# Two-layer hybrid trunk: four normalised half tiles and the first attention's queries and keys transposed by transfers, the end of attention reordered, half of one scaling moved to ScalarE

## The chip, the cores and the metric

The kernel runs on one core of a Trainium2 chip. The metric is device time in microseconds (us) of one execution. The kernel before has a median of 1316.64 us over three runs (1316.31 to 1316.8). The execution that the profiler recorded took 1317.49 us; the span from its first to its last instruction is 1315.7 us.

Five engines appear: PE (TensorE, matrix products and transposes), DVE (VectorE), ACT (ScalarE), POOL (GpSimd) and SP (SyncE), whose queue issues nearly all transfers. Each engine executes its own instructions in their program order, and waits at an instruction until what that instruction needs is there.

## The reference

Two layers over 256 tokens of width 1024 in float32. Each layer is a half-weighted SwiGLU block, an attention block with three branches, a second SwiGLU block and a gated embedding. Cut to what matters here:

```python
for i in range(DEPTH):                                    # DEPTH = 2
    h = h + 0.5 * swiglu(rms_norm(h, norm_g[i, 0]), ffn1_wi[i], ffn1_wo[i])
    z = split_cols(rms_norm(h, norm_g[i, 1]) @ w_in[i], IN_SPLITS)
    # z: aq, ak, av | bq, six key/value sets, gates | cq, ck, cv | ga, gb, gc
    ya = diff_attention(aq, ak, av, ...)                  # 4 heads, two maps each
    yb = nsa_attention(bq, ..., sigmoid(bgate), ...)      # compressed + selected + window
    yc = swa_sink_attention(cq, ck, cv, ...)              # window of 128 with sinks
    merged = (sigmoid(ga) * (ya @ w_branch[i, 0]) + sigmoid(gb) * (yb @ w_branch[i, 1])
              + sigmoid(gc) * (yc @ w_branch[i, 2]))
    h = h + merged @ w_out[i]
    h = h + 0.5 * swiglu(rms_norm(h, norm_g[i, 2]), ffn2_wi[i], ffn2_wo[i])
    h = h + sigmoid(rms_norm(h, norm_g[i, 3]) @ w_ple_gate[i]) * (p[i] @ w_ple[i])
return rms_norm(h, final_norm)
```

## The kernel before

The 256 tokens are two row tiles, t = 0 and 1, of 128 tokens. A float32 product is made of three products of shorter operands: each operand is split into a high part and a remainder (`split`, ACT writes the high part at L249, DVE the remainder at L244), and `mul3` (L256 to L258) multiplies high by high, high by remainder and remainder by high. So every pair of a 128-deep block of the left side and 512 columns of weights costs PE three instructions.

**Weights** are streamed in pieces of 128 x 1024 (`load`, L355). One piece is a transfer into one of four `raw` buffers (SP, L361), ACT's `wh` and DVE's `wl`, in six buffers each. All pieces of the program stand in one queue in the order of their use, and a product that reaches a piece has the next two fetched too. `product` (L388) takes tile 0 through its blocks and tile 1 eight blocks behind it; a 1024-deep product of 512 columns has eight blocks, so there tile 0 is done before tile 1 begins. When a tile's sum is complete, `done` is traced at raised priority.

**The order of the instructions** comes from a planner: the program is traced in order, and the planner then simulates the engines and issues, for each engine, what is ready first by its own estimates, with the trace order (moved forward for what is traced at raised priority) as the preference. Buffers of a tag are handed out as they come free. `keep_in_program_order` pins an instruction behind what has been traced before it on its engine. Slow side work (the attention branches) is written as generators in `Flow`: `flow.tick()`, once for every block of a product, lets each lane advance by its pace, and `flow.join` runs a side to its end.

**Transposes.** What is to be the left side of a product must be transposed. In most places PE does it: `transposes` (L264) turns 128 x 128 blocks into a PSUM bank of the tag `tp` (three banks), and ACT and DVE split the result from there. `Norm.turn` does so for half a row tile (four blocks) of `h` after each half of a residual, multiplying by the norm's weight on the way (L429, L430). `toT` (L876) does it for queries and keys: in `done_a` (L941) for the first attention, four blocks for each of two products `A0`, `A1` and each row tile. The SwiGLU blocks use `turn_by_dma` (L529) for their inner activations: ACT copies the float32 tile into two planes of 16-bit halves (`cut`, L535), SP issues a transposing transfer into `flip` (L536), and `collect` puts the halves together again (L541) on ACT or DVE, five steps of the block's line of products later.

**The output products of a SwiGLU block** (`fo`, `run` in `outer`, L810) are made in two halves of 512 columns, c = 0 and 1; behind each half and row tile `residual` (L465) adds to `h`, turns the half tile for the next norm and adds up its squares.

**Attention's end**, in the generators of `attention` and `branch`: for the last branch (b) the gate products of both halves are made, the branch's side is joined for tile 0, `tile(0)` makes the two products with `yB[0]` and mixes them into `merged`, turns them (`mt`, L1333) and splits them into `mT[0]`; then the side is joined to its end and `tile(1)` does the same for tile 1. Then come the output products `wo`, half 0 for both tiles, half 1 for both tiles. Product banks are two of the tag `mm` and two of the tag `s`.

**Scaling in branch b**: after the softmax, `first` in `attend_b` multiplies each head's probabilities by a number per row on DVE (L1228).

Of the kernel before, what the change touches and what calls it, by code (L numbers as in the profile page):

```python
# [11 lines left out]
F32R = mybir.dt.float32r  # L12
# [9 lines left out]
NT = SEQ // 128  # L22
# [11 lines left out]
FIRST, LAST = 7, 3  # L34
SPLIT = 16
POINTS = (5, 8, 11, 14, 18, 21)
PACE_A, PACE_B, PACE_C = 0.75, 0.72, 0.6
# [170 lines left out]
def trunk(ctx: ExitStack, tc: tile.TileContext, a: dict, out: bass.AP, index: list):  # L208
# [60 lines left out]
    class Weights:  # L269


        def __init__(self, width, pieces, per, push=True):
            self.width, self.per, self.pieces = width, per, pieces
            self.tiles, self.at = [None] * len(pieces), [None] * len(pieces)
            if push:
                for j in range(len(pieces)):
                    self.push(j)

        def push(self, j):
            self.at[j] = len(queue)  # L280
            queue.append(lambda: self.tiles.__setitem__(j, load(*self.pieces[j], 2 if self.at[j] < 2 else 1)))

# [88 lines left out]

    def streamed(i, name, width, push=True):
        p, c = where[i, name]
        return Weights(width, [(a["wst"][p + j], SUB) for j in range(c)], SUB // width, push)

# [31 lines left out]
    class Norm:  # L407
# [9 lines left out]
        def turned(self, t, k, src, pin=False):  # L417
# [47 lines left out]
    def residual(norm, c, scale, final=False):  # L465

        s = slice(512 * c, 512 * c + 512)

        def done(t, ps):
            nc.vector.scalar_tensor_tensor(h[:, t, s], ps, scale(t), h[:, t, s], op0=ALU.mult, op1=ALU.add)  # L470
# [58 lines left out]
    def turn_by_dma(pool, src, m):  # L529


        cut = stage("cut").bitcast(U16)[:, :256 * m]
        flip = pool.tile([128, 2, 4, 128], U16, tag="flip", bufs=4, name="flip")
        flip = flip.rearrange("p w a b -> p (w a) b")[:, :2 * m]
# [10 lines left out]
    def ffn(i, n, norm, after, aside=None):  # L545
# [4 lines left out]
        def begin():  # L550
            nonlocal pool
            pool = phase("ffn")
            for t in range(NT):
                gT[t] = pool.tile([128, 2, NF, 128], F32R, name=f"gT{t}")
# [307 lines left out]
    def attention(i, norm, after):  # L862
# [3 lines left out]
        def begin():  # L866
            nonlocal pool
            pool = phase("attn")
            wide[0] = False
            for t in range(NT):  # L870
                merged[t] = pool.tile([128, D], F32, name=f"merged{t}")
# [4 lines left out]
        def toT(dst, t, blocks, srcs):  # L876

            ps = tp_bank("qt")
            transposes(ps, srcs)
            v = ps[:, :len(srcs) * 128].rearrange("p (k q) -> p k q", q=128)  # L880
            ts = slice(t * 128, (t + 1) * 128)
            split(dst[:, 0, blocks, ts], dst[:, 1, blocks, ts], v)

        def scores(name, q, qb, t, key):
# [56 lines left out]
        def done_a(m):  # L941
            def done(t, ps):
# [4 lines left out]
                nc.vector.tensor_scalar(sb[:, 256:], ps[:, 256:], norm.r(t), None, op0=ALU.mult)  # L947
                toT(qk[m], t, slice(0, 4), [sb[:, 128 * k:128 * k + 128] for k in range(4)])
            return done
# [61 lines left out]
        def done_bk(t, ps):  # L1011
# [3 lines left out]
            for c in range(2):  # L1015
# [3 lines left out]
                nc.scalar.activation(dst[:, :, 0, :], src, AF.Copy, scale=norm.r(t))  # L1019
                nc.vector.tensor_scalar(dst[:, :, 1, :], src, norm.r(t), None, op0=ALU.mult)  # L1020
                srcs = [sb[:, k * 128:(k + 1) * 128] for k in range(4)]
# [7 lines left out]
                else:  # L1029
                    toT(kB[0], t, slice(0, 4), srcs)  # L1030

# [14 lines left out]
        def done_q(dst, name):  # L1046
            def done(t, ps):
# [3 lines left out]
                nc.scalar.activation(sb, ps, AF.Copy, scale=norm.eighth(t))  # L1051
                toT(dst[0], t, slice(0, 4), [sb[:, 128 * k:128 * k + 128] for k in range(4)])
            return done
# [144 lines left out]
        def attend_b():  # L1198
            bnd, y_ps = {}, {}

            def first(u):
# [25 lines left out]
                for j in range(n):  # L1227
                    nc.vector.tensor_scalar(pr[j], pr[j], st[:, 2 * n + j:2 * n + j + 1], None, op0=ALU.mult)  # L1228
                yield
                return p  # L1230

            def second(u, p):
# [12 lines left out]
                if ss[-1] == 1:  # L1245
# [4 lines left out]
                    weighted(y_ps[g, t], vc[0][:, 0], T.rearrange("p x j q -> p x (j q)"), False, True)  # L1250
                    gather(yB[t], y_ps[g, t], g)
                    readyB[t] += 1
# [7 lines left out]
        def done_ck(t, ps):  # L1260
# [6 lines left out]
            nc.scalar.activation(dst[:, :, 0, :], src, AF.Copy, scale=norm.r(t))  # L1267
            nc.vector.tensor_scalar(dst[:, :, 1, :], src, norm.r(t), None, op0=ALU.mult)
            toT(kC[0], t, slice(0, 2), [sb[:, 0:128], sb[:, 128:256]])
            values(vC[0][:, t], ps[:, 128:256], norm.r(t))  # L1270
# [43 lines left out]
        def branch(b, yT, side, last=False):  # L1314
# [69 lines left out]
        def start(name, side, pace, lane=0):  # L1384
            sides[name] = flow.start(side, pace, lane)

        yield lambda: start("a", attend_a(), PACE_A)
        yield project("Ck", done_ck, 256)
        yield project("Cq", done_q(qC, "qC"))
        yield project("Bk", done_bk)  # L1390
        yield lambda: start("c", attend_c(), PACE_C)
        wbv = a["wbv"][i]
# [3 lines left out]
        yield from branch(0, yA, "a")  # L1396
        yield second_weights
        yield lambda: start("b", attend_b(), PACE_B)
        w1 = streamed(i, "w1", 256)
# [120 lines left out]

    opened = []

    def phase(name):
# [3 lines left out]
        opened.append(stack)  # L1527
        return stack.enter_context(tc.tile_pool(name=name, bufs=1, reuse_waits="tile"))

# [73 lines left out]
```

## Time and profile before

| | |
|---|---|
| median of three runs | 1316.64 us (1316.31 to 1316.8) |
| profiled execution | 1317.49 us, span 1315.7 us |
| PE busy | 1300.9 us, 99% of the span, 6306 instructions |
| PE's weight loads | 1072.7 us, 82% |
| DVE busy | 1098.3 us, 83%, 1778 instructions |
| ACT busy | 890.6 us, 68%, 1412 instructions |
| POOL busy | 29.1 us, 2% |
| chain that ended last | PE 95%, DVE 2%, issue 1%, ACT 1% |
| DMA | 259.55 MB, mean 197 GB/s |

A row of the groups view names the line, the engine and the operation, then what is written and read (`out<-in`), the shape and the number of instructions; behind the bar stand the busy time, the mean time of one and the time that the engine sat idle before them, with what ended it. The busy time of PE counts overlapping instructions once. A matmul of 512 columns shows 0.39 us from its start to its modelled end, but the next one starts 0.23 us after it, so what an instruction costs PE is read from the starts of its neighbours in the timeline.

### The profile page before, as it was taken

The numbers are of one execution on the slowest core, as the hardware profiler recorded it, in microseconds if no ns is written. First come the engines' busy times: TensorE is split into PE (matmuls) and PEld (weight loads), VectorE is DVE, ScalarE is ACT, GpSimd is POOL, SyncE is SP. The second block draws the span as 40 slices with busy tenths as digits, with TensorE's granted clock in tenths as the row PEclk, the third lists the DMA queues.
The fourth block names the chain that finished last, engine by engine and source line by source line (L and its number), as shares of the span: only waits on it lengthen the run. The fifth ranks groups of instructions, "written<-read, shape, count | busy, mean of one in ns | idle before, by whom it ended". The sixth has DMA issues, their size and how long they took to land.

```text
span 1315.7 us, 18006 instructions
## 1 busy us (share of the span) xinstructions
PE 1300.9 (99%) x6306; PEld 1072.7 (82%) x6306; DVE 1098.3 (83%) x1778; ACT 890.6 (68%) x1412; POOL 29.1 (2%) x46
## 2 busy tenths in 40 slices
PE   9999999999999999999999999999999999999997
PEld 7888888887887788888888888888888878888886
DVE  7878976768979799997799999677688888999975
ACT  6777555658857577874667875566695656877654
POOL 0000000000000000000000000000000000000000
PEclk9999999999999999999999999999999999999999
DMA  8778775346653567786666796744556436677762
GB/s 309 231 227 267 206 223 203 116 161 188 217 165 109 169 184 241 220 224 214 205 193 228 203 248 206 243 154 153 176 159 218 158 96 210 202 212 232 216 223 81
DMA packets 120283, 259.55 MB, mean 197 GB/s; under 512 B 54774, under 2 KB 60278, under 8 KB 120192
## 3 DMA queue, kind: packets, MB, share of 16 engines
q1 hardware_dynamic: 117232, 248.38, 60.7%
q0 software_dynamic: 2528, 9.47, 2.1%
q8 instruction: 49, 0.80, 0.3%
q10 hardware_dynamic: 432, 0.56, 0.1%
q14 instruction: 42, 0.34, 0.1%
HBM read 245.75 MB, written 1.08 MB: 188 GB/s over the span
## 4 chain that ended last, share of the span: by engine, by line
PE 95%; DVE 2%; issue 1%; ACT 1%; DMA 0%; SPq 0%; POOLq 0%; POOL 0%; DVEq 0%; ACTq 0%
PE ff L258 8%; PE ff L257 8%; PE ff L256 8%; PE fo L257 5%; PE fo L258 5%; PE fo L256 5%; PE p L256 4%; PE p L257 4%; PE p L258 4%; PE gate L258 3%; PE gate L256 3%; PE gate L257 3%; PE s L895 2%; PE A L258 2%; PE A L256 2%; PE A L257 2%
## 5 line engine op out<-in xcount | busy, mean ns | idle before, releaser
L249 ACT ACTIVATE wh<-raw 128x1024 fp32r<-128x1024 f32 (+2 forms) x430 | 446.8, 1049 | 208.2 <-DMA raw<-in_wst 63.9
L244 DVE TENSOR_TENSOR wl<-raw,wh 128x1024 fp32r<-128x1024 f32 (+2 forms) x430 | 514.4, 1211 | 85.4 <-ACT wh L249 82.0
L257 PE MATMUL ff<-wl,nT 128*128 128x512 f32 x480 | 187.8, 393 | 0.0
L258 PE MATMUL ff<-wh,nT 128*128 128x512 f32 x480 | 187.4, 392 | 0.2 <-DVE nT L244 0.2
L256 PE MATMUL ff<-wh,nT 128*128 128x512 f32 x480 | 179.8, 394 | 0.6 <-ACT nT L430 0.6
L257 PE MATMUL fo<-wl,gT 128*128 128x512 f32 x304 | 117.7, 390 | 0.0
L258 PE MATMUL fo<-wh,gT 128*128 128x512 f32 x304 | 117.6, 391 | 0.0
L256 PE MATMUL fo<-wh,gT 128*128 128x512 f32 x304 | 114.9, 390 | 0.0
L256 PEld LDWEIGHTS ff<-wh,nT 128*128 128x128 f32 x480 | 90.9, 189 | 20.7 <-ACT nT L430 1.6
L258 PEld LDWEIGHTS ff<-wh,nT 128*128 128x128 f32 x480 | 90.9, 189 | 19.6 <-DVE nT L244 0.8
L257 PEld LDWEIGHTS ff<-wl,nT 128*128 128x128 f32 x480 | 90.9, 189 | 19.5 <-DVE wl L244 0.8
L256 PE MATMUL gate<-wh,nT 128*128 128x512 f32 x192 | 76.8, 400 | 0.0
L257 PE MATMUL gate<-wl,nT 128*128 128x512 f32 x192 | 76.2, 397 | 0.0
L258 PE MATMUL gate<-wh,nT 128*128 128x512 f32 x192 | 76.0, 396 | 0.0
L257 PEld LDWEIGHTS fo<-wl,gT 128*128 128x128 f32 x304 | 57.1, 188 | 12.3 <-DVE wl L244 0.5
L256 PEld LDWEIGHTS fo<-wh,gT 128*128 128x128 f32 x304 | 57.1, 188 | 11.8
L258 PEld LDWEIGHTS fo<-wh,gT 128*128 128x128 f32 x304 | 57.1, 188 | 11.7
L906 ACT ACTIVATE p<-p,st 128x128 f32<-128x128 f32 (+1 forms) x128 | 56.7, 446 | 6.3 <-DVE st L904 6.1
L535 ACT ACTIVATE cut<-gated 128x1024 uint16<-128x1024 uint16 (+1 forms) x48 | 46.1, 975 | 10.0 <-DVE gated L574 8.8
L244 DVE TENSOR_TENSOR wl<-x,wh 128x1024 fp32r<-128x1024 f32 x42 | 50.6, 1221 | 2.3 <-ACT wh L249 2.0
L249 ACT ACTIVATE wh<-x 128x1024 fp32r<-128x1024 f32 x42 | 43.7, 1049 | 6.3 <-DVE x L244 4.6
L257 PE MATMUL p<-wl,xs 128*128 128x512 f32 x112 | 43.6, 389 | 0.0
(377 smaller groups left out, 2719.6 us busy)
## 6 DMA issues: line engine op xcount, KB each, us to landing
raw<-in_wst SPq DMA_DIRECT2D x424, 512.0 KB, 4.4
y<-in_wst POOLq DMA_DIRECT2D x6, 1024.0 KB, 5.8
band<-table SPq DMA_DIRECT2D x10, 512.0 KB, 5.1
xy<-in_wst POOLq DMA_DIRECT2D x4, 512.0 KB, 4.0
raw<-in_wbv SPq DMA_DIRECT2D x4, 420.0 KB, 3.2
xt<-in_xt SPq DMA_DIRECT2D x4, 256.0 KB, 5.5
raw<-in_wst SPq DMA_DIRECT2D x4, 256.0 KB, 5.1
h<-in_x SPq DMA_DIRECT2D x2, 512.0 KB, 7.8
```

What stands on the lines that cost most here:

```text
L244: nc.vector.tensor_tensor(o, x, y, op=ALU.subtract)
L249: nc.scalar.activation(hi, src, AF.Copy)
L256: nc.tensor.matmul(ps, xh, wh, start=start, stop=False, **kw)
L257: nc.tensor.matmul(ps, xh, wl, start=False, stop=False, **kw)
L258: nc.tensor.matmul(ps, xl, wh, start=False, stop=stop, **kw)
L535: nc.scalar.activation(cut.rearrange("p (w n) -> p w n", w=2), halves(src)[:, :128 * m].rearrange("p n w -> p w n"), AF.Copy)
L895: nc.tensor.matmul(o, q[r, x, qb[m], t * 128:(t + 1) * 128], kk, start=x + y == 0, stop=x == 1)
L906: nc.scalar.activation(p[j], p[j], AF.Exp, bias=st[:, j:j + 1], scale=-1.0, accum_out=st[:, n + j:n + j + 1])
```

## The change

The diff has five parts. **(1)** `residual` calls the new `turn_late` for half 0 behind `fo` (norms with odd row numbers: two per layer, two row tiles each): `turn_by_dma` in place of PE's four transposes, and after eight ticks `collect` on ACT and the rest of the norm as before, from SBUF. **(2)** `done_a` calls the new `late_T`, which for `A0` and `A1` does the same with `collect` on DVE; all other callers get `toT` as before. `turned_all` joins these sides ahead of the branches. **(3)** In the last branch the gate of half 1 is made up to all but its last two blocks for tile 1; these two blocks follow the join for tile 1. The output products are traced in a new order, with two blocks of half 1 for tile 0 between the tiles of half 0, and the first two weight pieces of `wo` half 0 lie in buffers of the tag `blk` in place of `wh` and `wl`. `gather` of the last unit of branch b is traced at raised priority. **(4)** Every second scaling of L1228 runs on ACT. **(5)** In `done_bk` and `done_ck` the second copy of the keys is copied from the first one in place of being scaled from PSUM again. The flips of attention use buffers of the tag `th`.

```diff
+TURNS = ('A0','A1')
+ON_DVE = TURNS
+QWAIT = 8
+SHARE = 2
+LEFT = 2
+APART = ((0, 1), ())
+WAIT = 8
+LATE_ON = False
...
-    def load(src, n, parts=1):
+    def load(src, n, parts=1, apart=False):
         raw = base.tile([128, SUB], F32, tag="raw", bufs=RAWS, name="raw")
-        hi = base.tile([128, SUB], F32R, tag="wh", bufs=WBUFS, name="wh")
-        lo = base.tile([128, SUB], F32R, tag="wl", bufs=WBUFS, name="wl")
+        if apart:
+            both = base.tile([128, 2, SUB], F32R, tag="blk", bufs=6, name="wb")
+            hi, lo = both[:, 0], both[:, 1]
+        else:
+            hi = base.tile([128, SUB], F32R, tag="wh", bufs=WBUFS, name="wh")
+            lo = base.tile([128, SUB], F32R, tag="wl", bufs=WBUFS, name="wl")
...
+        def turn_late(self, t):
+            collect = turn_by_dma(current[0], h[:, t, :512], 4)
+            def side():
+                for _ in range(WAIT):
+                    yield
+                with tc.high_priority(offset=150):
+                    self.turned(t, 0, collect(LATE_ON).rearrange("p k q -> p (k q)"))
+                yield
+            flow.start(side(), 1.0, ("nt", t))
...
             if final:
                 finish(t, 0, 512)
+            elif c == 0 and norm.row % 2:
+                norm.turn_late(t)
             else:
                 norm.turn(t, c)
...
+        def late_T(name, dst, t, n, sb):
+            if name not in TURNS:
+                return toT(dst, t, slice(0, n), [sb[:, 128 * k:128 * k + 128] for k in range(n)])
+            collect = turn_by_dma(pool, sb, n)
+            def side():
+                for _ in range(QWAIT):
+                    yield
+                ts = slice(t * 128, (t + 1) * 128)
+                split(dst[:, 0, :n, ts], dst[:, 1, :n, ts], collect(name in ON_DVE))
+                yield
+            turning.append(flow.start(side(), 1.0, ("qt", name, t)))
...
-                toT(qk[m], t, slice(0, 4), [sb[:, 128 * k:128 * k + 128] for k in range(4)])
+                late_T(f"A{m}", qk[m], t, 4, sb)
...
-                nc.vector.tensor_scalar(dst[:, :, 1, :], src, norm.r(t), None, op0=ALU.mult)
+                nc.vector.tensor_copy(dst[:, :, 1, :], dst[:, :, 0, :])
...
                 for j in range(n):
-                    nc.vector.tensor_scalar(pr[j], pr[j], st[:, 2 * n + j:2 * n + j + 1], None, op0=ALU.mult)
+                    of = st[:, 2 * n + j:2 * n + j + 1]
+                    if j % SHARE:
+                        nc.scalar.activation(pr[j], pr[j], AF.Copy, scale=of)
+                    else:
+                        nc.vector.tensor_scalar(pr[j], pr[j], of, None, op0=ALU.mult)
...
             if last:
-                for c in range(2):
-                    yield gated(c, both[c][0])
+                yield gated(0, both[0][0])
+                wg = streamed(i, f"g{'abc'[b]}1", 512)
+                gate_ps = [None] * NT
+                def gates(t, ks):
+                    for k in ks:
+                        if k == 0:
+                            gate_ps[t] = product_bank(f"gate{t}")
+                        mul3(gate_ps[t], *norm.lhs(t, k), *wg(k), k == 0, k == NK - 1)
+                        flow.tick()
+                    if ks[-1] == NK - 1:
+                        with tc.high_priority(offset=150):
+                            both[1][0](t, gate_ps[t])
+                yield lambda: gates(0, range(NK))
+                yield lambda: gates(1, range(NK - LEFT))
                 ws = [streamed(i, f"br{b}{c}", 512) for c in range(2)]
...
                 yield lambda: tile(0)
                 yield lambda: flow.join(sides[side])
+                yield lambda: gates(1, range(NK - LEFT, NK))
                 yield lambda: tile(1)
...
-        for c in range(2):
-            yield product(lambda t, k: (mT[t][:, 0, k, :], mT[t][:, 1, k, :]), NK, after(c), "wo", streamed(i, f"wo{c}", 512))
+        done = [after(c) for c in range(2)]
+        ws = [streamed(i, f"wo{c}", 512, apart=APART[c]) for c in range(2)]
+        def out():
+            ps = {}
+            for c, t, ks in ((0, 0, range(NK)), (1, 0, range(2)), (0, 1, range(NK)), (1, 0, range(2, NK)), (1, 1, range(NK))):
+                for k in ks:
+                    if k == 0:
+                        ps[c, t] = product_bank(f"wo{t}")
+                    mul3(ps[c, t], mT[t][:, 0, k, :], mT[t][:, 1, k, :], *ws[c](k), k == 0, k == NK - 1)
+                    flow.tick()
+                if ks[-1] == NK - 1:
+                    with tc.high_priority(offset=150):
+                        done[c](t, ps[c, t])
+        yield out
```

More of the change, by code (lines that the diff above doesn't have):

```diff
@@ L35 @@
 SPLIT = 16
+TURNS = ('A0','A1')
[6 more added lines that the diff above has]
+LATE_ON = False
+FLIPS = ["flip"]
 POINTS = (5, 8, 11, 14, 18, 21)
@@ L269, in trunk, with __init__ @@
     class Weights:
-        def __init__(self, width, pieces, per, push=True):
-            self.width, self.per, self.pieces = width, per, pieces
+        def __init__(self, width, pieces, per, push=True, apart=()):
+            self.width, self.per, self.pieces, self.apart = width, per, pieces, apart
             self.tiles, self.at = [None] * len(pieces), [None] * len(pieces)
@@ L280, in push @@
             self.at[j] = len(queue)
-            queue.append(lambda: self.tiles.__setitem__(j, load(*self.pieces[j], 2 if self.at[j] < 2 else 1)))
+            queue.append(lambda: self.tiles.__setitem__(j, load(*self.pieces[j], 2 if self.at[j] < 2 else 1, j in self.apart)))
         def __call__(self, k):
@@ L370, in trunk, with streamed @@
         pos += c
-    def streamed(i, name, width, push=True):
+    def streamed(i, name, width, push=True, apart=()):
         p, c = where[i, name]
-        return Weights(width, [(a["wst"][p + j], SUB) for j in range(c)], SUB // width, push)
+        return Weights(width, [(a["wst"][p + j], SUB) for j in range(c)], SUB // width, push, apart)
     def last_product(lhs, nk, done, name, w):
@@ L532, in turn_by_dma @@
         cut = stage("cut").bitcast(U16)[:, :256 * m]
-        flip = pool.tile([128, 2, 4, 128], U16, tag="flip", bufs=4, name="flip")
+        flip = pool.tile([128, 2, 4, 128], U16, tag=FLIPS[0], bufs=4, name="flip")
         flip = flip.rearrange("p w a b -> p (w a) b")[:, :2 * m]
@@ L552, in begin @@
             pool = phase("ffn")
+            FLIPS[0] = "flip"
             for t in range(NT):
@@ L868, in begin @@
             pool = phase("attn")
+            FLIPS[0] = "th"
             wide[0] = False
@@ L882, in toT, with turned_all @@
             split(dst[:, 0, blocks, ts], dst[:, 1, blocks, ts], v)
+        turning = []
+        def late_T(name, dst, t, n, sb):
[9 more added lines that the diff above has]
+            turning.append(flow.start(side(), 1.0, ("qt", name, t)))
+        def turned_all():
+            while turning:
+                flow.join(turning.pop(0))
         def scores(name, q, qb, t, key):
@@ L1029, in done_bk @@
                 else:
-                    toT(kB[0], t, slice(0, 4), srcs)
+                    late_T("Bk", kB[0], t, 4, sb)
         def values(v, ps, scale):
@@ L1051, in done @@
                 nc.scalar.activation(sb, ps, AF.Copy, scale=norm.eighth(t))
-                toT(dst[0], t, slice(0, 4), [sb[:, 128 * k:128 * k + 128] for k in range(4)])
+                late_T(name, dst[0], t, 4, sb)
             return done
@@ L1250, in second @@
                     weighted(y_ps[g, t], vc[0][:, 0], T.rearrange("p x j q -> p x (j q)"), False, True)
-                    gather(yB[t], y_ps[g, t], g)
+                    with tc.high_priority(offset=150 if g == t == 1 else 0):
+                        gather(yB[t], y_ps[g, t], g)
                     readyB[t] += 1
@@ L1267, in done_ck @@
             nc.scalar.activation(dst[:, :, 0, :], src, AF.Copy, scale=norm.r(t))
-            nc.vector.tensor_scalar(dst[:, :, 1, :], src, norm.r(t), None, op0=ALU.mult)
-            toT(kC[0], t, slice(0, 2), [sb[:, 0:128], sb[:, 128:256]])
+            nc.vector.tensor_copy(dst[:, :, 1, :], dst[:, :, 0, :])
+            late_T("Ck", kC[0], t, 2, sb)
             values(vC[0][:, t], ps[:, 128:256], norm.r(t))
@@ L1385, in start @@
             sides[name] = flow.start(side, pace, lane)
+        yield turned_all
         yield lambda: start("a", attend_a(), PACE_A)
@@ L1390, in attention @@
         yield project("Bk", done_bk)
+        yield turned_all
         yield lambda: start("c", attend_c(), PACE_C)
@@ L1397, in attention @@
         yield second_weights
+        yield turned_all
         yield lambda: start("b", attend_b(), PACE_B)
@@ L1519, in setup @@
         yield
-    opened = []
+    opened, current = [], []
     def phase(name):
@@ L1527, in phase @@
         opened.append(stack)
-        return stack.enter_context(tc.tile_pool(name=name, bufs=1, reuse_waits="tile"))
+        current[:] = [stack.enter_context(tc.tile_pool(name=name, bufs=1, reuse_waits="tile"))]
+        return current[0]
     norms = [Norm(n) for n in range(4 * DEPTH + 1)]
```

## The prediction

> **What bounds the kernel now.** I read the page first (engines, groups), then who waited for whom on PE, then PE's timeline at the places that the change touches.
>
> ```profile
> PE 1300.9 (99%) x6306; PEld 1072.7 (82%) x6306; DVE 1098.3 (83%) x1778; ACT 890.6 (68%) x1412; POOL 29.1 (2%) x46
> ```
>
> PE's own waits (time in all, times, longest):
>
> ```profile
> PE wo L256 <- ACT mT L252: 1.4, 2, 0.7
> PE mt L264 <- DVE pT L244: 1.2, 2, 0.6
> ...
> PE gl L1097 <- DVE c_sb L1090: 0.5, 2, 0.3
> ...
> PE wo L256 <- ACT wh L249: 0.5, 2, 0.2
> ```
>
> PE is busy for 1300.9 of 1315.7 us, and nearly all of the remaining 14.8 us lie before the first product and behind the last. The waits inside the program are small; the three around `wo` and `mt` lie at attention's end and are 3.1 us over both layers. So the time is the number of PE instructions times their spacing, and an edit helps only if it takes instructions or waits off PE.
>
> The spacing is read from starts, and so is what a group of four transposes costs:
>
> ```profile
> 179.65 0.62 PE L258 MATMUL fo<-wh,gT 128*128 128x512 f32 x2
> 180.10 0.39 PE L256 MATMUL fo<-wh,gT 128*128 128x512 f32 x1
> 180.34 0.60 PE L264 MATMUL nt<-ident,h 128*128 128x128 f32 x4
> 180.69 0.48 PE L256 MATMUL fo<-wh,gT 128*128 128x512 f32 x1
> ...
> 199.88 0.40 PE L258 MATMUL A<-wh,nT 128*128 128x512 f32 x1
> 200.12 0.60 PE L264 MATMUL qt<-ident,stage 128*128 128x128 f32 x4
> 200.47 0.48 PE L256 MATMUL A<-wh,nT 128*128 128x512 f32 x1
> ...
> 204.91 0.39 PE L257 MATMUL A<-wl,nT 128*128 128x512 f32 x1
> 205.14 0.38 PE L264 MATMUL qt<-ident,stage 128*128 128x128 f32 x2
> 205.28 0.48 PE L258 MATMUL A<-wh,nT 128*128 128x512 f32 x1
> 205.60 0.39 PE L256 MATMUL A<-wh,nT 128*128 128x512 f32 x1
> 205.83 0.38 PE L264 MATMUL qt<-ident,stage 128*128 128x128 f32 x2
> 205.96 0.48 PE L257 MATMUL A<-wl,nT 128*128 128x512 f32 x1
> ```
>
> Two products start 0.45 us before the next, so one takes 0.23. With four transposes between, the next product starts 0.59 us after the last one (180.10 to 180.69, 199.88 to 200.47): the group costs 0.36 us. Split into pairs it costs 0.14 (204.91 to 205.28, less 0.23) and 0.13 (205.60 to 205.96), 0.27 together.
>
> **The change part by part.** Durations are from the profiled execution (1317.49 us, span 1315.7), 0.85 us above the median of the runs; the sum of differences is taken off the median.
>
> *Norm halves.* Two layers, two SwiGLU blocks, two row tiles: 8 groups leave PE, 8 x 0.36 = **-2.9 us**.
>
> *Queries and keys of the first attention.* 2 products x 2 row tiles x 2 layers: 8 groups. In the first layer one is whole and three are in pairs; taking the second layer alike, 2 x (0.36 + 3 x 0.27) = **-2.3 us**. The bounds are all split (-2.2) and all whole (-2.9).
>
> What takes their place runs on ACT, SP and DVE (the view of one tile: shortest, median and longest in ns; the groups; two stretches of the first layer):
>
> ```profile
> L535 ACT ACTIVATE cut<-gated x48: 614/1042/1061, 33.7 to 1222.9; 128x1024 uint16<-128x1024 uint16 x40, 128x512 uint16<-128x512 uint16 x8
> L536 SPq DMA_TRANSPOSE flip<-cut x48: 1189/1239/4823, 34.8 to 1224.3; - x48
> DMA to landing us min/median/max: 3.0/4.2/8.1
> ```
>
> ```profile
> L541 ACT ACTIVATE whole<-flip 128x1024 uint16<-128x1024 uint16 x24 | 32.0, 1364 | 2.9 <-DMA flip<-cut 2.7
> ```
>
> ```profile
> L541 DVE COPY gw<-flip x8: 741/752/756, 125.1 to 1215.7; 128x1024 uint16<-128x1024 uint16 x8
> ```
>
> ```profile
> 157.00:188.00 31.00, 31.00 (x143) 25.60 (x142) 24.04 (x37) 16.24 (x21) 0.15 (x1) 1.00 0.66 204
> 188.00:224.00 36.00, 36.00 (x172) 29.17 (x169) 23.45 (x34) 19.57 (x28) 3.02 (x2) 1.00 0.63 209
> ```
>
> Each late norm half adds 1.04 us of `cut` and 1.36 of `collect` on ACT; each late query tile 1.04 on ACT and 0.75 on DVE. The two stretches (columns: PE, PEld, DVE, ACT, POOL, clock, DMA share, GB/s) hold two of the former and four of the latter: ACT goes to 16.2 + 4.8 = 21.0 of 31 and 19.6 + 4.2 = 23.8 of 36 us, DVE in the second to 23.5 + 3.0 = 26.5 of 36. So idle time of ACT and DVE covers them. SP issues 16 more transfers of 1.24 us, in order with the weights; the same transfers, 48 of them, already stand in that queue. DMA is at 0.66 and 0.63.
>
> The data isn't late for PE either:
>
> ```profile
> 175.32 0.75 DVE L470 SCALAR_TENSOR_TENSOR h<-fo,stats,h 128x512 f32<-128x512 f32 x1 [0.85 <-PE fo L258]
> ...
> 194.02 0.60 PE L264 MATMUL nt<-ident,h 128*128 128x128 f32 x4
> ...
> L947 DVE TENSOR_SCALAR stage<-A,stats x4: 474/476/479, 198.2 to 213.0; 128x256 f32<-128x256 f32 x4
> ...
> 237.52 0.45 PE L895 MATMUL s<-qkA 64*128 64x128 f32 x4
> ```
>
> The later half tile is in `h` at 176.1. With cut (1.04), the slowest landing (8.1), collect (1.36) and some 2 us of scaling and splitting it is there at 188.6; tile 1 reads it from 194.0 (I take the group at 194.02 as the border between the row tiles), 5.4 us later. The last query tile is scaled at 213.5 and is there at 213.5 + 1.04 + 8.1 + 0.75 + 1.3 = 224.7; the scores that read `A1` begin at 237.5.
>
> What can be late is the engine: `collect` holds ACT or DVE until its flip lands, with the next weight splits queued behind it, and PE waits for those. In the trace 24 collects on ACT waited 2.9 us in all. Sixteen more at that rate are 1.9 us of a blocked engine; I give PE **+0.5 us** of it, as it has some weights ahead, with 0 and +1.9 as the ends.
>
> The Trainium skill speaks against this part: the page "VectorE: DVE Perf Modes" ("Rules for kernel authors") says to transpose 128x128 on TensorE if a PSUM destination is fine, and "The three transpose paths" there sets 390 ns against 1309 ns for the transfer. The trace has the same order (0.09 us of PE for a block, 3.0 us at least for a flip of four), and by that rule as it stands the transposes would stay on PE, both terms above with their +0.5 would drop out, and 1314.4 us would be left.
>
> *Attention's end.* PE's waits are these (first layer):
>
> ```profile
> 424.90 0.63 PE L264 MATMUL mt<-ident,merged 128*128 128x128 f32 x4 [0.58 <-DVE pT L244]
> ...
> 432.42 0.50 PE L256 MATMUL wo<-wh,mT 128*128 128x512 f32 x1 [0.24 <-ACT wh L249]
> ...
> 438.34 0.60 PE L264 MATMUL mt<-ident,merged 128*128 128x128 f32 x4
> 439.63 0.50 PE L256 MATMUL wo<-wh,mT 128*128 128x512 f32 x1 [0.69 <-ACT mT L252]
> ```
>
> Two blocks of `wo` half 1 (6 products, 1.4 us) can stand where 0.69 us are lost for `mT[1]`. The two weight pieces in `blk` leave the six `wh` buffers to others, which takes away the wait of 0.24 us. The wait for a `tp` bank at 424.90 isn't touched by either; the two held-back gate blocks (1.4 us) would fill it only if the planner sees that wait, which it put there without. I take the waits for `mT` and `wh`: **-1.9 us** over both layers, -3.1 if all three go.
>
> On the other side, the unfinished gate sum holds one of the two `mm` banks, so the second product of `tile(0)` must wait until the first has been read:
>
> ```profile
> 419.88 0.69 DVE L1328 SCALAR_TENSOR_TENSOR th<-th,br 128x512 f32<-128x512 f32 x1 [0.37 <-PE br L258]
> ```
>
> That is 0.37 + 0.69 = 1.1 us in a layer if nothing else is ready, +2.1 for both. PE's timeline there has products and transposes of branch b between those of `br`, so I count it at nothing and keep +2.1 as the far end. The new `wb` tiles take two of six `blk` buffers; I count norm 1's tile 0, which is no longer read, and the freed keys as giving the room.
>
> *Scaling and key copies.* Of 64 scalings 32 move:
>
> ```profile
> L1228 DVE TENSOR_SCALAR p<-p,st 128x128 f32<-128x128 f32 (+1 forms) x64 | 15.7, 313 | 0.3
> ...
> L1295 ACT ACTIVATE p<-p,st 128x128 f32<-128x128 f32 (+1 forms) x32 | 11.9, 445 | 0.0
> ...
> 342.27 0.85 DVE p L1228 x4
> ```
>
> DVE loses 32 x 0.31 = 10.0 us, ACT gains 32 x 0.445 = 14.2. Neither bounds, but the chain of waits goes through four of these scalings just ahead of the `c_sb` for which PE waits 0.5 us in all: **-0.3 us**, between -0.5 and 0. The key copies change 12 operations of DVE (0.48 us each if they are as long as L947's above, the same kind of scaling from PSUM) and PE's waits name none of them: nothing.
>
> **Sum:** -2.9 - 2.3 + 0.5 - 1.9 - 0.3 = -6.9. The median becomes 1316.64 - 6.9 = **1309.7 us**.
>
> **The rivals.**
>
> *The end gives nothing back.* The `mm` bank is awaited in both layers (+2.1) and the waits stay: -2.9 - 2.3 + 0.5 - 0.3 + 2.1 = -2.9, 1313.7 us. For it: only two banks, and the planner places work by estimates, as the wait at 424.90 shows. Against it: branch b's ready work. Chance 0.20.
>
> *The weights are the next bound.* Where PE gets shorter, the splits aren't faster, so PE's saved 5.2 us come back as waits for `wh` and `wl`; only the end's 1.9 and the 0.3 remain: 1314.4 us. Against it:
>
> ```profile
> ACT wh L249 <- PE fo L258: 8.7, 8, 2.6
> ```
>
> Between 156 and 192 us ACT waits for PE to free the buffers, not the reverse. Chance 0.10.
>
> *Late collects stop the weights: slower.* The planner puts a collect where it expects the flip. If it expects the fastest landing (3.0 us) and the median one comes (4.2), each of 16 collects blocks its engine for 1.2 us; with no weights ahead PE loses 19.2: 1316.64 - 6.9 - 0.5 + 19.2 = 1328.4 us. It turns into a loss from 7.4 / 16 = 0.46 us per collect. For it: the gap to the collect is eight ticks, 8 x 3 x 0.23 = 5.5 us, against five lines of products in the SwiGLU blocks, and the row just shown means that weights come only as fast as buffers are freed. Against it: ACT's 24 collects lost 0.12 us each. Chance 0.07. The skill's rule above would be a case of this one.
>
> *The change doesn't do what it says:* the planner leaves the attention's end as it is, with neither gain nor loss there: 1316.64 - 5.0 = 1311.6 us. This lies in my own range.
>
> **How the numbers follow.** The forecast has 0.63. Its own ends are -2.9 - 2.9 - 3.1 - 0.5 = -9.4 (1307.2) and -2.9 - 2.2 + 1.9 = -3.2 (1313.4). Below it I add 2.7 us, since attention is planned anew and a switch from products to scores costs PE 0.32 - 0.23 = 0.09 us:
>
> ```profile
> 223.60 0.39 PE L258 MATMUL A<-wh,nT 128*128 128x512 f32 x1
> 223.92 0.43 PE L895 MATMUL s<-qkA 64*128 64x128 f32 x3
> ```
>
> Thirty switches fewer would be that much. Above it the range takes in the first two rivals: 1304.5 to 1315.5. About 0.2% (2.6 us) is what a measurement can tell from no change: faster holds for the forecast and the first rival, 0.83; the second rival is the same, 0.10; slower 0.07.
>
> **What would show it.** Right: 80 `nt` and 56 `qt` instructions on PE in place of 112 and 88, 64 flips, PE's products back to back at 0.23 us through `fo` and `A`, no wait for `mT` or `wh` at the first `wo`. Wrong: PE waiting for `wh` or `wl` behind a collect; ACT or DVE idle before `whole` by more than 0.5 us each; PE waiting at `br` for DVE's L1328; more than some 1 us of new waits among the scores and transposes of the attention branches.

## The result and the profile after

The changed kernel takes 1307.67 us (median of 4 runs, 1307.16 to 1309.08), the kernel before 1316.72 beside it (4 runs, 1316.31 to 1317.3): ratio 0.9932 with a 95% interval of 0.9919 to 0.9945, 9.05 us less. The forecast was 1309.7 us within 1304.5 to 1315.5. The profiled execution of after took 1308.18 us, with a span of 1306.4.

The engines in the page of after, and then all of PE's waits (time, times, longest):

```profile
PE 1294.4 (99%) x6242; PEld 1068.1 (82%) x6242; DVE 1092.9 (84%) x1754; ACT 923.6 (71%) x1468; POOL 28.6 (2%) x46
```

```profile
PE warm L1633 <- DVE idle L1628: 1.5, 1, 1.5
PE ff L265 <- ACT nT L443: 1.2, 1, 1.2
PE ff L267 <- DVE nT L253: 0.6, 1, 0.6
PE ff L266 <- DVE wl L253: 0.2, 1, 0.2
```

PE has 64 instructions fewer, the 32 transposes of norm halves and 32 of queries and keys. The four waits left lie at the very start, ahead of the first `fo`. All that before had behind it (for `mT`, `wh`, `pT`, `c_sb`) are gone. The other signs of being right came too: 80 `nt`, 56 `qt`, 64 flips.

The clearest measure is a stretch that leaves the program's head out. I take it from the start of the first `fo` to the start of the last `pg`, the last product of the program. The head, all that comes before, has the same order of PE instructions in all 14 traces and yet takes between 127.3 and 129.1 us, while later stages in which two kernels have the same plan mostly agree within 0.1. An exception: from the first `fo` to the first `A` four kernels take 59.91 to 59.93 us, and e4 below, with the same plan there, 60.53. There is one trace of each kernel. The row of such a stretch gives its length, PE's busy time with the number of its instructions, and then PEld, DVE, ACT, POOL, the clock, the DMA share and GB/s. Length less busy time is PE's idle time. First before, then after:

```profile
128.61:1306.93 1178.32, 1174.27 (x5781) 971.03 (x5779) 994.83 (x1645) 795.43 (x1294) 23.31 (x34) 1.00 0.61 191
```

```profile
129.11:1297.54 1168.43, 1168.43 (x5717) 966.67 (x5715) 989.64 (x1621) 828.73 (x1350) 22.80 (x34) 1.00 0.64 196
```

So 9.9 us go: 4.05 of idle time, all there was, and 5.84 of busy time. After's head was 0.5 us longer, which leaves 9.4 between the two executions.

What runs on the other engines in place of the transposes, in after: the view of the tile `flip`, the group of its collects on ACT, and the longest single wait for a flip in ACT's timeline.

```profile
L562 SPq DMA_TRANSPOSE flip<-cut x64: 1188/1238/5019, 35.3 to 1254.6; - x64
DMA to landing us min/median/max: 2.5/4.0/7.8
```

```profile
L567 ACT ACTIVATE whole<-flip 128x1024 uint16<-128x1024 uint16 x32 | 43.0, 1364 | 20.8 <-DMA flip<-cut 20.7
```

```profile
173.59 1.05 ACT L258 ACTIVATE wh<-raw 128x1024 fp32r<-128x1024 f32 x1
179.03 1.38 ACT L567 ACTIVATE whole<-flip 128x1024 uint16<-128x1024 uint16 x1 [4.39 <-DMA flip<-cut]
```

Durations and landings are close to those of before. What is new is ACT's wait: 20.7 us in nine collects, where before had 2.7. In the third fence ACT stands still for 4.39 us behind a weight split, and PE shows no wait there.

At attention's end PE's timeline (first layer) has no gap:

```profile
425.56 0.39 PE L267 MATMUL br<-wh,yB 128*128 128x512 f32 x1
425.78 0.39 PE L265 MATMUL wo<-wb,mT 128*128 128x512 f32 x1
...
438.04 0.60 PE L273 MATMUL mt<-ident,merged 128*128 128x128 f32 x4
438.39 0.48 PE L266 MATMUL wo<-wl,mT 128*128 128x512 f32 x1
```

The first `wo` product comes at the usual 0.22 us behind branch work, and where before waited 0.69 us for `mT` a `wo` product follows the transposes directly.

### The profile page after: what moved, and what is told of

The parts are those of the page before. It is cut to its first block, busy times and chain, and to the rows that moved or that the text cites. A ratio compares the mean times of both kernels' runs of the same rounds, so it can differ in the third digit from the quotient of the medians.

```text
span 1306.4 us, 17953 instructions
## 1 busy us (share of the span) xinstructions
PE 1294.4 (99%) x6242; PEld 1068.1 (82%) x6242; DVE 1092.9 (84%) x1754; ACT 923.6 (71%) x1468; POOL 28.6 (2%) x46
## 4 chain that ended last, share of the span: by engine, by line
PE 98%; issue 0%; DMA 0%; DVE 0%; ACT 0%; SPq 0%; POOLq 0%; POOL 0%; DVEq 0%; ACTq 0%
PE ff L267 8%; PE ff L265 8%; PE ff L266 8%; PE fo L266 5%; PE fo L265 5%; PE fo L267 5%; PE p L265 4%; PE p L266 4%; PE p L267 4%; PE gate L265 3%; PE gate L267 3%; PE gate L266 3%; PE s L942 3%; PE A L266 2%; PE br L265 2%; PE A L265 2%
## 5 line engine op out<-in xcount | busy, mean ns | idle before, releaser
L253 DVE TENSOR_TENSOR wl<-raw,wh 128x1024 fp32r<-128x1024 f32 (+1 forms) x426 | 510.3, 1213 | 94.9 <-ACT wh L258 93.4
L258 ACT ACTIVATE wh<-raw 128x1024 fp32r<-128x1024 f32 (+1 forms) x426 | 441.6, 1048 | 153.3 <-DMA raw<-in_wst 55.2
L567 ACT ACTIVATE whole<-flip 128x1024 uint16<-128x1024 uint16 x32 | 43.0, 1364 | 20.8 <-DMA flip<-cut 20.7
```

The source lines that it names most:

```text
L253: nc.vector.tensor_tensor(o, x, y, op=ALU.subtract)
L258: nc.scalar.activation(hi, src, AF.Copy)
L567: tc.keep_in_program_order(nc.vector.tensor_copy(to, of) if late else nc.scalar.activation(to, of, AF.Copy))
```

## The experiments

The theory was that of the prediction: each part gives what its instructions and waits cost on PE. The rivals were that the late collects cost PE time, that the parts pay only together, and that the gains come from the changed order rather than from the work removed. Kernels named u, w and a are after with something undone or altered; those named e are before with one or two parts added.

### The norm halves

```diff
-            elif c == 0 and norm.row % 2:
-                norm.turn_late(t)
```

> The changed kernel with one part undone: the eight norm halves are turned by PE again. Theory (a count of PE's instructions): eight groups of four transposes come back at 0.36 us each, so 1307.7 + 2.9 = 1310.6 us, and the 20.7 us that ACT waited for flips fall to the 3 us of the kernel before without any gain from it. Rival (the waits of ACT for the flips cost PE time): less than 2.9 comes back, about 1308.5. Second rival (the four output stages of the SwiGLU blocks got 4.6 us shorter in the traces): all of that comes back, 1312.3 us.

Measured 1311.05 us against 1317.59, ratio 0.9951 [0.9939, 0.9964]. Its stretch:

```profile
129.05:1301.26 1172.21, 1172.21 (x5749) 969.52 (x5747) 991.91 (x1622) 812.50 (x1336) 23.41 (x34) 1.00 0.63 194
```

Neither it nor after has idle time, and the 32 transposes take 3.78 us, 0.47 for each of the eight groups. By the ratios of the times it is 0.0019 x 1316.7 = 2.5 us, with an uncertainty of some 2.4. The prediction had 0.36 a group. What it left out is in the row of before's timeline that comes after the one it used (180.69):

```profile
181.00 0.40 PE L257 MATMUL fo<-wl,gT 128*128 128x512 f32 x1
```

The product behind the transposes also keeps PE for 181.00 - 180.69 = 0.31 us instead of 0.23, so a group costs 0.36 + 0.08 = 0.44.

Turning the even norms' first halves as well:

```diff
-            elif c == 0 and norm.row % 2:
+            elif c == 0:
```

> The changed kernel with late turns for half 0 of the even norms too, behind wo and behind the first layer's gated embedding: six more groups leave PE. Theory (a turn off PE saves 0.5 us, as the eight in the output stages did by 3.8 us of stage time): 3.0 us less, 0.9909 of before. Rival (ACT and DVE have no room at attention's end, and a flip of 4 us is late for the block that follows): no gain or a loss there, 0.9932 or above.

Measured 1309.35 against 1317.35, ratio 0.9936 [0.9924, 0.9949]: no different from after. Its stretch, and a wait that it has on PE behind the first `fo`:

```profile
127.90:1297.23 1169.33, 1168.05 (x5693) 963.10 (x5691) 989.83 (x1622) 840.83 (x1364) 24.13 (x34) 1.00 0.65 198
```

```profile
PE ff L265 <- ACT wh L258: 0.9, 1, 0.9
```

It has 24 instructions fewer, and 0.9 us of its 1.3 us of idle time are a wait for a weight split of ACT. Why busy time falls by 0.4 us only is not settled.

### The queries and keys

```diff
-TURNS = ('A0','A1')
+TURNS = ()
```

> The changed kernel with the first attention's queries and keys turned by PE again. Theory (count): 2 x (0.36 + 3 x 0.27) = 2.3 us come back, 1310.0 us. Rival: the A stages of the two traces differ by only 0.5 and 0.1 us, so no more than 0.6 comes back, 1308.3 us.

Measured 1308.54, ratio 0.9932 [0.9919, 0.9944]: the same as with this part. The other way round, before with this part alone. Written as an edit of after, it has the old end as in u3 below and this (the last line twice, in `done_bk` and `done_ck`):

```diff
-SHARE = 2
+SHARE = 1
...
-            elif c == 0 and norm.row % 2:
-                norm.turn_late(t)
...
-                nc.vector.tensor_copy(dst[:, :, 1, :], dst[:, :, 0, :])
+                nc.vector.tensor_scalar(dst[:, :, 1, :], src, norm.r(t), None, op0=ALU.mult)
```

> The kernel before with the first attention's queries and keys turned by transfers alone. Theory (count of PE's instructions): 2.3 us faster, 0.9983 of before. Rival (the scores start earlier and are cut into more pieces between other products, which costs PE what the transposes gave, as in the changed kernel with this part undone): within 0.5 us, 0.9996 to 1.0004.

Measured 1316.81 against 1317.56, ratio 0.9995 [0.9987, 1.0004]: no change. The stretches, first u2, then e3:

```profile
127.81:1296.69 1168.88, 1168.18 (x5749) 968.42 (x5747) 984.94 (x1613) 822.41 (x1343) 21.92 (x34) 1.00 0.63 194
```

```profile
127.88:1305.67 1177.79, 1173.20 (x5748) 968.32 (x5747) 1000.98 (x1654) 803.01 (x1304) 23.31 (x34) 1.00 0.62 193
```

The part takes 0.45 us off after's stretch and 0.53 off before's. Busy time hardly falls, though 32 instructions go (after has 0.25 us more of it than u2). The scores show why. After, where they begin:

```profile
213.28 0.39 PE L265 MATMUL A<-wh,nT 128*128 128x512 f32 x1
213.60 0.44 PE L942 MATMUL s<-qkA 64*128 64x128 f32 x3
213.96 0.50 PE L266 MATMUL A<-wl,nT 128*128 128x512 f32 x1
214.29 0.39 PE L267 MATMUL A<-wh,nT 128*128 128x512 f32 x1
...
215.55 0.33 PE L942 MATMUL s<-qkA 64*128 64x128 f32 x2
...
217.16 0.33 PE L942 MATMUL s<-qkA 64*128 64x128 f32 x2
...
223.08 0.33 PE L942 MATMUL s<-qkA 64*128 64x128 f32 x2
...
224.25 0.43 PE L942 MATMUL s<-qkA 64*128 64x128 f32 x3
```

Before has the same twelve in two runs, three at 223.92 and nine here:

```profile
224.98 0.28 PE L258 MATMUL Ck<-wh,nT 128*128 128x256 f32 x1
225.19 0.77 PE L895 MATMUL s<-qkA 64*128 64x128 f32 x9
225.89 0.38 PE L256 MATMUL Ck<-wh,nT 128*128 128x256 f32 x1
226.11 0.28 PE L257 MATMUL Ck<-wl,nT 128*128 128x256 f32 x1
```

Three scores cost PE 214.29 - 213.28 - 2 x 0.23 = 0.55 us; nine cost 1.13 - 2 x 0.12 = 0.89 (a `Ck` product of 256 columns takes 0.12). So one more score is 0.06 us and a run by itself some 0.38. Other runs of after fit this price: two scores between `A` products cost 0.46 us (0.50 by the price), twelve between `Ck` products 1.11 (1.10). With the queries turned by transfers the planner cuts the twelve scores into five runs. Counted over the program, PE has 54 runs of scores in after against 44 in u2 and in before, and 52 in e3. Ten runs at 0.38 are 3.8 us. The transposes taken off are, by the prediction's rows with the product behind each group (0.31 or 0.32 instead of 0.23), 0.44 + 6 x 0.23 = 1.8 us a layer, 3.6 in all. The two nearly cancel, as measured. This is an estimate, since other runs change in number too (transposes of probabilities from 55 in u2 to 52); taken from each start to the next one in the stretch, the scores take 2.4 us more in after than in u2, and the transposes `qt` 2.0 less. That the planner cuts because the data now comes at other times is likely, but it wasn't tried.

### The late collects

```diff
-WAIT = 8
+WAIT = 24
```

> The changed kernel with 24 ticks in place of 8 ahead of the late norm halves' collects, so that ACT reaches them after the flips have landed. Theory (weights ahead of PE cover ACT's 20.7 us of waits): the waits fall to about 3 us and the time stays within 0.5 us of the changed kernel's 0.9932 of before. Rival (the waits cost PE time): faster by 2 us or more, 0.9917.

Measured 1306.67 against 1317.56, ratio 0.992 [0.9906, 0.9934], which overlaps that of after. And with no gap:

```diff
-WAIT = 8
+WAIT = 0
```

> The changed kernel with no ticks ahead of the late norm halves' collects. Theory (ACT's waits for flips are covered): ACT waits at least as long as the 20.7 us before, and the time stays at 0.9932 of before within 0.5 us. Rival (the slower case of the prediction: blocked splits stop PE): PE waits for wh or wl in the output products of the SwiGLU blocks, and the time rises by more than 2 us, above 0.9947.

Measured 1308.83 against 1317.35, ratio 0.9933 [0.9921, 0.9946]. ACT's wait for flips in w1 and in w2, and then their stretches in the same order:

```profile
ACT whole L567 <- DMA flip<-cut: 3.8, 4, 1.8
```

```profile
ACT whole L567 <- DMA flip<-cut: 16.6, 9, 3.0
```

```profile
127.86:1295.99 1168.13, 1168.13 (x5717) 966.54 (x5715) 988.81 (x1619) 827.40 (x1348) 22.11 (x34) 1.00 0.64 196
```

```profile
128.60:1297.04 1168.44, 1168.28 (x5716) 966.48 (x5715) 990.84 (x1621) 828.26 (x1350) 23.38 (x34) 1.00 0.65 196
```

ACT's blocked time falls from 20.7 us to 3.8 and PE's stretch by 0.3. The shorter gap was to lengthen the wait and didn't (16.6 us): there the collect also goes out at other times. Between 3.8 and 20.7 us of blocked ACT, PE loses 0.3 us at most.

### Attention's end and the scaling

The new end without the share of ACT, and the share without the new end, each undone in after:

```diff
-SHARE = 2
+SHARE = 1
```

> The changed kernel with all scalings of branch b on DVE. Theory: only PE's 0.5 us of waits for c_sb hang on it, 0.3 us come back, 1308.0 us, not to be told from 1307.7. Rival: DVE is the late engine between 300 and 345 us of each layer and ten us of DVE work are worth over 1 us, above 1308.7 us.

Measured 1310.45 against 1317.59, ratio 0.9946 [0.9933, 0.996].

```diff
-                yield gated(0, both[0][0])
...
-                yield lambda: gates(1, range(NK - LEFT))
+                for c in range(2):
+                    yield gated(c, both[c][0])
...
-                yield lambda: gates(1, range(NK - LEFT, NK))
...
-        yield out
+        for c in range(2):
+            yield product(lambda t, k: (mT[t][:, 0, k, :], mT[t][:, 1, k, :]), NK, after(c), "wo", streamed(i, f"wo{c}", 512))
```

(`gather` at its usual priority and no `blk` pieces either.)

> The changed kernel with attention's end as before (both gates whole ahead of the join, the output products half by half, no pieces in blk buffers, the last gather without raised priority). Theory (the waits that PE showed there): 3.1 us of waits come back, 1310.8 us, with PE waiting for mT, wh and a tp bank again. Rival (the bank held by the unfinished gate sum costs what the filling gains): about 1307.7 us. Second rival (a new plan of the whole attention is worth more than the waits): above 1312 us.

Measured 1316.89, ratio 0.9992 [0.9983, 1.0]: with the old end nearly the whole gain of after is gone. Then each alone in before, the new end first (part 3 of the change; in short):

```diff
-                for c in range(2):
-                    yield gated(c, both[c][0])
+                yield gated(0, both[0][0])
...
+                yield lambda: gates(0, range(NK))
+                yield lambda: gates(1, range(NK - LEFT))
...
+                yield lambda: gates(1, range(NK - LEFT, NK))
```

> The kernel before with the new end of attention alone. Three prices stand against each other: PE's waits there in the trace of before, 3.1 us (0.9976 of before); the stage from the last compressed product to the next SwiGLU block, 1.9 and 2.0 us shorter in the changed kernel's trace, 3.9 us (0.9970); what undoing the end cost the changed kernel, 8.3 us (0.9937). If the parts work on their own, one of the first two holds; if the end's worth were what its undoing showed, the third.

Measured 1317.49 against 1317.56, ratio 0.9999 [0.999, 1.0008].

```diff
-                    nc.vector.tensor_scalar(pr[j], pr[j], st[:, 2 * n + j:2 * n + j + 1], None, op0=ALU.mult)
+                    of = st[:, 2 * n + j:2 * n + j + 1]
+                    if j % SHARE:
+                        nc.scalar.activation(pr[j], pr[j], AF.Copy, scale=of)
+                    else:
+                        nc.vector.tensor_scalar(pr[j], pr[j], of, None, op0=ALU.mult)
```

> The kernel before with half of branch b's scaling on ACT alone. Theory (it relieves DVE): PE's 0.5 us of waits for c_sb go, 0.9997 of before, or 1.9 us as its undoing in the changed kernel showed, 0.9986. Rival (with the old end the moved scaling makes the end longer: the trace of the changed kernel with the old end has 1.8 us more than before in each layer from the last compressed product to the next block): slower by 2 to 4 us, 1.0015 to 1.0030.

Measured 1321.15 against 1317.56, ratio 1.0028 [1.0017, 1.004]: slower. So the end gives nothing alone and the scaling costs 3.6 us alone; if they added up, both would be slower than before. The last run of this group has both diffs in before:

> The kernel before with the new end and the shared scaling together, all transposes on PE. If the two were independent, their single results add: 0 + 3.6 us, slower, 1.0027 of before. Theory (they need each other: the stage from the last compressed product to the next SwiGLU block takes 116.1 us with neither, 115.3 with the new end alone, 117.6 with the sharing alone, 114.1 with both in the changed kernel): 2 x 1.95 us less there and some 0.4 us more in each following block, 3.1 us faster, 0.9976.

Measured 1313.49 against 1317.35, ratio 0.9971 [0.9959, 0.9982], 3.9 us faster. The stretch, and behind it PE's largest waits, of u4, u3, e1, e2 and e4 in turn:

```profile
127.98:1299.57 1171.59, 1168.93 (x5717) 966.94 (x5715) 994.64 (x1652) 818.89 (x1317) 21.05 (x34) 1.00 0.64 195
```

```profile
PE br L265 <- ACT yB L258: 2.0, 2, 1.0
```

```profile
128.19:1306.22 1178.03, 1171.76 (x5716) 965.93 (x5715) 989.23 (x1621) 827.79 (x1350) 22.63 (x34) 1.00 0.64 194
```

```profile
PE wo L266 <- DVE wl L253: 1.5, 2, 0.8
```

```profile
127.31:1307.12 1179.81, 1173.87 (x5781) 971.09 (x5779) 994.91 (x1646) 794.11 (x1296) 23.34 (x34) 1.00 0.61 191
```

```profile
PE ff L259 <- DVE wl L246: 1.8, 2, 1.0
PE yb L1152 <- ACT pcT L251: 1.7, 2, 0.9
PE p L259 <- DVE wl L246: 0.9, 1, 0.9
```

```profile
127.33:1309.73 1182.40, 1175.14 (x5781) 970.21 (x5779) 987.93 (x1613) 803.90 (x1326) 24.08 (x34) 1.00 0.61 190
```

```profile
PE br L257 <- ACT th L1327: 1.5, 2, 0.8
PE wo L258 <- DVE wl L245: 1.5, 2, 0.8
```

```profile
128.05:1302.83 1174.78, 1172.88 (x5781) 970.43 (x5779) 989.09 (x1614) 806.89 (x1328) 23.34 (x34) 1.00 0.62 192
```

```profile
PE br L259 <- ACT th L1334: 1.2, 2, 0.7
```

PE's idle time in the stretch (length less busy, in us) makes the table of two by two:

```
                     neither   new end   share   both
added to before        4.05      5.94     7.26   1.90
within after             -       2.66     6.27   0.00
```

The sharing alone adds idle time, and both together take away 2.15 us of what before has. The new end alone looks worse here than it is. Of its 5.94 us, 1.75 are two waits for weight remainders in the SwiGLU block behind the second layer's attention (0.91 at 1176.50, 0.84 at 1178.77), which the first layer hasn't; without them it has about as much as before. u3 has 1.0 us of the same.

So I also measured the stage that the two parts touch, from the first `cmp` (the compressed products) of a layer to the first `fo` of the next block, between starts in PE's timeline (us):

```
                 before    e1      e2      e4      u3      u4    after
first layer      242.17  242.09  244.58  240.06  245.14  242.55  240.94
second layer     242.25  244.14  244.24  240.48  246.35  242.70  241.14
```

The new end alone changes the first layer by 0.1 us and the second, without those two waits, by 0.1 as well. The sharing alone adds 2.0 to 2.4 us in each layer, and both together take 1.8 to 2.1 off, 3.9 in all, as the times say. In after, without the share it is 1.6 us longer in each layer, with the old end 4.2 and 5.2 (1.0 of it the weight waits just named).

The waits show what is exchanged. With the end alone, PE stops wanting `mT` and `wh`; instead `mt` waits 0.70 us in each layer for `pT` (0.58 before), and `yb` 0.86 for `pcT`, ahead of which ACT splits the two new `wb` pieces (2.02 us from 423.25 on, `pcT` at 425.14). In after without the share `br` waits for `yB`, 1.0 us in a layer. The share takes work of DVE out of branch b's units, and in the new end the last of these units is what is late; that this is why the two need each other is an inference.

With the share alone, `wo` waits 0.76 us a layer for a weight split, `mt` 0.7 for `merged`, and `br` 0.75 for `th`, the gate that ACT makes. This last wait is not at attention's end but at branch c's products with `yC` (at 354.95 and 1003.70). ACT isn't held up by the scalings right there: its last four before this gate end at 347.87, and what stands just ahead of `th` (354.23) is a weight split that waited 0.48 us for its transfer and took from 353.26 to 354.32. So what differs at that point is the order on ACT; why the planner chose it was not found.

### Further groups to the transfers

```diff
-TURNS = ('A0','A1')
+TURNS = ('A0','A1','Ck','qC','Bk','qB')
```

> The changed kernel with the queries and keys of all three branches turned by transfers: 56 more transposes leave PE. Count: 14 groups at 0.36 us, or 0.27 where they are in pairs, 3.8 to 5.0 us less, 0.9894 to 0.9903 of before. Rival (as with the first attention, the plan moves and cuts the scores and gives it back): within 1 us of 0.9932, or slower where the branches start later.

Measured 1331.98 against 1317.35, ratio 1.0105 [1.009, 1.0121]: slower than before by 14.6 us. Its stretch, from the slowest of its four runs (1335.32), and its largest wait on PE:

```profile
127.95:1324.82 1196.87, 1179.04 (x5661) 971.27 (x5659) 997.58 (x1637) 843.19 (x1367) 22.83 (x34) 0.99 0.65 195
```

```profile
PE s L942 <- DVE st L951: 4.3, 3, 2.7
```

Another 56 instructions leave PE, which now stands idle for 17.8 us in many places (the wait shown is 4.3 of it), and its busy time is 10.6 us longer than in after, with a lower clock (0.99, more below). The rule that the prediction cited from the Trainium skill ("VectorE: DVE Perf Modes", "Rules for kernel authors": 128x128 on TensorE where PSUM will do) holds for these groups; for the norm halves the stretch of u1 speaks against it.

## Why the prediction was right

Predicted terms beside the change of PE's stretch:

```
step                   predicted   measured   by
norm halves              -2.9        -3.8     u1 (1172.21 to 1168.43)
queries and keys         -2.3        -0.5     u2, e3
late collects            +0.5         0       w1, w2 (0.3 at most)
end and scaling          -2.2        -3.5     e4 (1178.32 to 1174.78)
key copies                0           -       not run by itself
sum                      -6.9        -7.8, and -9.9 for the whole change
```

By the stage from `cmp` to `fo` the end and scaling are -3.9: the stretch of e4 has the 0.6 us of its longer first stage in it.

**Norm halves:** the mechanism held and the size was off. The group's cost was read up to the start of the next product; the 0.08 us that this product adds was missing, and with it the term is -3.5. The remaining 0.3 us are not assigned.

**Queries and keys:** this step failed. It counted the transposes taken off PE and took the rest of PE's order as given. What the runs showed in its place is ten more runs of scores. The prediction did know the price of such a switch (0.09 us, from the start of the first score alone) and put it in the range; a whole run costs four times that.

**Late collects:** what the slower rival needs did come, ACT blocked for 2.3 us in each of nine collects, against its break-even of 0.46; it was also one of the prediction's signs of being wrong. Its price did not come: w1 takes nearly all of that away and PE gains 0.3 us. The reason given, "some weights ahead", fits, as PE waits for no weight while ACT stands still, and the 0 end of the range should have been taken.

**Attention's end:** the waits for `mT` and `wh` went, and the wait for `pT` at 424.90 too, which gives the -3.1 end of the bounds. But it is not the end that gives it: alone it moves the time by nothing, and leaves as much idle time as there was. The step costed the waits it saw and not those that come next, and these, for `pT` and `pcT` in branch b, were not in the sum. The opening text put nearly all of PE's idle time ahead of the first product and behind the last; 4.05 us of it lie between, and the waits it listed are most of that. The rival of the awaited bank named L1328, DVE's reading of `br`; no kernel here shows that wait at `br`. In e2 and e4 it is branch c's `br` that waits, for ACT's reading of the gate (`th`), and after does not.

**Scaling:** predicted at -0.3 within -0.5 and 0, it is +4.1 alone (1178.32 to 1182.40) and -3.2 with the new end (1171.59 to 1168.43, u4 to after). The term failed: it priced one wait, for `c_sb`, and took the rest of the order as given. DVE gave up its 32 scalings as planned (1645 to 1613 instructions in e2's stretch), so the count was right; that it is worth anything depends on the other part.

**What is left:** the parts as run give -7.8 of -9.9. Of the 2.1 us between, 1.9 are the idle time that e4 still has and after has not. Of this, 1.2 are branch c's `br` waiting for `th` (0.58 and 0.65 us); what freed it in after was not found. Another piece is a wait of `ya` for `pT` in the first layer, which before shows at 267.71:

```profile
267.71 0.33 PE L256 MATMUL ya<-va,pT 128*128 128x128 f32 x1 [0.51 <-ACT pT L249]
```

It is there in e1 to e4, which all scale the second keys from PSUM, and in none of the kernels with copied keys except a1, which has 0.5 us of waits of `ya` in its second layer. So the copies are the likely cause of that 0.5 us; they were not run by themselves.

That the total lies in the range is partly luck. It came out 3.0 us short of the stretch's -9.9 (some 2 us short by the times) because the missing gain of the queries (+1.8) was met by the norm halves (-0.9), the end with the scaling (-1.3), the collects (-0.5) and the rest that no run takes apart (-2.1).

## What to carry to other kernels

When one engine is busy for 99% of the span and the order is made by a planner, price a removed group up to the second product behind it, and ask how the planner will cut the work that follows: an extra run of scores cost nearly as much here (0.38 us) as four transposes (0.44). Cost a stall's removal together with whatever is late next, because two edits can each be worth nothing or less and be worth 4 us together. And leave the program's head out when kernels are compared by their traces, where it differs by more than the edits are worth.

## What the hardware showed that I had not expected

In a1 the granted clock fell after pauses of PE far shorter than those I had thought of. A row of its timeline and then four stretches of the first layer (after the start and end: length, PE, PEld, DVE, ACT, POOL, clock):

```profile
287.00 2.35 PE L942 MATMUL s<-kC,qC 64*128 64x128 f32 x12 [1.11 <-DVE st L951]
```

```profile
284.00:288.00 4.00, 2.52 (x19) 2.32 (x20) 4.00 (x21) 3.75 (x20) 0.69 (x1) 0.95 0.92 300
288.00:292.00 4.00, 4.00 (x21) 3.40 (x20) 2.68 (x16) 4.00 (x20) 0.00 (x0) 0.50 0.71 215
292.00:296.00 4.00, 4.00 (x20) 3.69 (x20) 3.20 (x15) 4.00 (x11) 0.00 (x0) 0.70 0.04 12
296.00:300.00 4.00, 4.00 (x20) 3.30 (x18) 3.13 (x6) 4.00 (x11) 0.00 (x0) 1.00 0.40 131
```

In the first stretch PE was idle for 1.48 us of 4, 1.11 of them at one wait; the clock was 0.50 in the next and is at 1.00 again in the fourth. So a wait was paid again in slower work: where the clock is at 0.50 in the second layer (952.00 to 956.00), `gate` products start 0.43 us apart instead of 0.23. In three other places of a1 the clock fell too (to 0.57 in 260:264, 0.73 in 924:928, 0.50 in 944:948), at single waits of 2.2, 2.1 and 2.7 us. The Trainium skill ("TensorE: Matmul & The Clock Gate", "Why this matters for your kernels") warns of gaps over some 3 us; in this trace shorter ones, in the stretch shown with score products between them, were followed by the drop. In the other kernels, whose single waits in the long stretch were 1.0 us at most, its clock is 1.00. How much idle time is needed was not measured.
